# Delta rule of a hybrid decoder: two substitution steps a bank, merges of all heads and chunks at once, gate folded into the output norm

## The chip, the cores and the metric

One NeuronCore of one Trainium2 chip. The metric is the device time of one launch in microseconds, the median over several runs. The kernel is written in Bass with Tile: the author gives the order of the program, and Tile's scheduler places every instruction in its engine's queue, the earlier ones of the program first where several could go, and adds the semaphores. On the chip each engine works through its queue in that order.

## The reference

A decoder trunk of two layers, 256 tokens, width 1024, float32. A layer is a half-step SwiGLU, a mixer of three branches side by side, and another half-step SwiGLU. The mixer's branches are a forgetting attention (8 heads), a latent attention (8 heads) and a gated delta rule (8 heads of 64). The delta rule, per head and chunk of 64 tokens, cut to what matters here:

```
m     = strict_lower(k_beta @ k.T * decay)
t_inv = inverse of (I + m)              # unit lower triangle, 64 x 64
w, u  = t_inv @ (k_beta * exp(gc)), t_inv @ v_beta
o     = recurrence over the chunks with w, u and a 64 x 64 state
o     = rmsnorm(o, dn_o_norm) * silu(z)
x    += W_out(sig(gA) * (A @ W_A) + sig(gB) * (B @ W_B) + sig(gC) * (o @ W_C))
```

## The kernel before, in words

All weights come from HBM in pieces of 512 KB through `wchunk` (L158): SP starts the load of `raw` (L163), ScalarE rounds it to `hi` (L164), VectorE takes the rest `lo` (through `tt`, L98), and `mm_w` (L177 to L179) or `mm_t` (L188 to L190) multiplies with three matmuls. Three buffers each of `raw`, `hi` and `lo` rotate. PSUM has four banks `m` for the projections, two `g` for the delta rule and two `a` for the attention heads; `turned` (L216) transposes an activation with L221 and splits it.

The function `mixer` gives its program in this order. First come the small projection with the gates' logits, the delta rule's six pieces of q, k and v, the decay sums (L459 to L486), the short convolutions, the norms of q and k, and the matrices N (L565) and Q (L569) for 8 heads and two blocks of 128 tokens, each with two chunks of 64. N holds the strict triangle; the inverse is built in three sizes:

- Substitution (L596 to L605). The 16x16 diagonal blocks of all heads and blocks stand side by side in `cn`. Step j spreads row j of each block over its 16 partitions with two matmuls with a selector (L599, L600), and VectorE multiplies and subtracts. The selected rows come from a copy of N that the steps don't change. After 15 steps `uc` has the inverses, and L609 writes them, masked to block diagonals, into `Um`, one half by VectorE and one by GpSimd.
- Merge of 16 to 32 (L614 to L626). Four groups of four heads, one after the other: a 32x32 transpose on VectorE (L617), four 128x128 matmuls (L620), the mask `lev16`, four matmuls (L625), a subtraction.
- Merge of 32 to 64 (L627 to L642). Two blocks times two halves: a transpose (L632), eight 32x32 matmuls (L635) at one position of the array, a negated copy on ScalarE (L637), eight matmuls (L640) at another, and a copy (L642).

Then the loop over the two blocks (L650 to L701): products with the triangle (L663, L668, L672), the state (L681, L657), the output (L686), then its norm (L693 to L701): `s2` is scaled twice by `rq`, brought to mean plus epsilon, `rsqrt` (L144) takes three Newton rounds, and `odn` is scaled.

Behind the delta rule in the program stand the query and key projections of the forgetting attention (`wft` 6 to 9), its values (`win[1]`), the delta rule's output gate `zt` (`win[2]`, L718 to L727, on ScalarE, VectorE and GpSimd), the latent attention's projections, the forgetting attention (8 heads, `attention` L356), the gates of branch 0, the latent attention, the gates of branches 1 and 2, and the merges of the branches 0, 1 and 2. Right before branch 2, GpSimd multiplies `odn` by `zt` (L823, L824); its operand is then transposed by L221. Then come `W_out` and the second SwiGLU.

Of the kernel before, what the change touches and what calls it, by code (L numbers as in the profile page):

```python
# [12 lines left out]
AF = mybir.ActivationFunctionType  # L13
ALU = mybir.AluOpType
# [4 lines left out]
P = 128  # L19
# [14 lines left out]

C_ID = 0
C_LV = C_ID + P
C_TRI = C_LV + P
C_KR = C_TRI + P
C_SELC = C_KR + P
C_IDC = C_SELC + 16  # L40
C_BM = C_IDC + 16
C_M01 = C_BM + 8
C_SEL = C_M01 + 2
C_SC = C_SEL + 30
NC_ = C_SC + 3

PAIRS_1 = (0, 1, 2, 3, 4, 5)
PAIRS_2 = (6, 7, 8, 9, 2, 3)
# [6 lines left out]
def trunk(ctx, tc, x_in, pos_in, cst_in, msk_in, sel_in, vec_in, hv_in, onorm_in, fin_in, bg_in,  # L55
# [20 lines left out]
    def bank(tag):  # L76
        return psum_of[tag].tile([P, 512], F32, name="bank_" + tag)
# [4 lines left out]
    def held(name, dt=F32):  # L82
        return pair(PAIR[name], dt)

    def single(name, dt=F32):
        return big.tile([P, 1024], dt, name=name)

    def w2(shape=(P, 512)):
        return wk.tile(list(shape), F32, name="w2", bufs=NW2)

    def g2(shape=(P, 512), dt=F32):
        return wk.tile(list(shape), dt, name="g2", bufs=NG2)
# [4 lines left out]
    def tt(eng, o, a, b, op):  # L97
        eng.tensor_tensor(out=o, in0=a, in1=b, op=op)  # L98
# [4 lines left out]
    def ts(o, a, s1, op0, s2=None, op1=None, eng=None):  # L103
        k = dict(op1=op1) if op1 is not None else {}
        (eng or V).tensor_scalar(out=o, in0=a, scalar1=s1, scalar2=s2, op0=op0, **k)
# [11 lines left out]
    for l in range(1, L):  # L117
        nc.scalar.dma_start(vec[l], vec_in[l])
    cc = lambda o, n: cst[:, o:o + n]
    ident, lev16, tri = cc(C_ID, P), cc(C_LV, P), cc(C_TRI, P)  # L120
    krsel = cst[0:64, C_KR:C_KR + P]
    idc, bm, m01 = cc(C_IDC, 16), cc(C_BM, 8), cc(C_M01, 2)
    invf, phase, sgn = [cc(C_SC + i, 1) for i in range(3)]
    bfc = const.tile([P, 3 * P + 16], BF16, name="bfc")
    msk = w2()
# [73 lines left out]
    def proj_t(ps, src, xs, kt=KD, k0=0, first=True, last=True):  # L199
        for q in range(0, kt, 2):  # L200
            w = wchunk(src[:, q * 512:(q + 2) * 512], 2, 512)
            mm_t(ps, w, 0, xs, k0 + q, 2, first and q == 0, last and q + 2 == kt)

    def two(tag):
        return [bank(tag) for _ in range(2)]
# [140 lines left out]
    def heads(ap):  # L346
        return ap.rearrange("p (h e) -> p h e", e=64)

    def hb(col, n=8, rows=slice(0, P)):
        return col[rows, :, None].broadcast_to([rows.stop - rows.start, n, 64])  # L350
# [38 lines left out]
    def mixer(l, norm, next_norm):  # L389
# [141 lines left out]
        rq = small([P, 2, 8], "rq")  # L531
        ts(rq, of(rs, 1), 0.125, ALU.mult)


        ps = bank("g")
        for p in range(4):
# [37 lines left out]
        for c in range(2):  # L574
# [1 line left out]
            for p in range(4):  # L576
                nc.tensor.transpose(ps[:, p * P:(p + 1) * P], vT[:, p, c * P:(c + 1) * P], ident)
            tt(V, heads(vr[:, c, :]), heads(ps), hb(irk[:, c, :]), ALU.mult)
        Ub = held("U")
        Um = [four(Ub[:, c, :]) for c in range(2)]  # L580

        cu = g2((P, 2, 16, 16))
        cn, uc = cu[:, 0], cu[:, 1]
# [10 lines left out]
        tt(V, cnl, flat(cn), cnh.bitcast(F32), ALU.subtract)  # L594
        G.tensor_copy(uc, idc[:, None, :].broadcast_to([P, 16, 16]))
        for j in range(15):  # L596
            ps = bank("g")
            sel = sel16[:, j, :]
            nc.tensor.matmul(ps[:, 0:256], sel, cnh, start=True, stop=False)  # L599
            nc.tensor.matmul(ps[:, 0:256], sel, cnl, start=False, stop=True)  # L600
            n = 15 - j
            row = ps[:, 0:256].rearrange("p (t i) -> p t i", t=16)[:, :, j + 1:16]
            tmp = cn[:, :, 0:n]
            tt(V, tmp, row, uc[:, :, j:j + 1].broadcast_to([P, 16, n]), ALU.mult)
            tt(V, uc[:, :, j + 1:16], uc[:, :, j + 1:16], tmp, ALU.subtract)  # L605
        for c in range(2):
            o = Um[c].rearrange("p h (b i) -> p h b i", i=16)
            u = uc[:, 8 * c:8 * c + 8, None, :].broadcast_to([P, 8, 8, 16])
            tt(V if c == 0 else G, o, u, bm[:, None, :, None].broadcast_to([P, 8, 8, 16]), ALU.mult)  # L609


        groups = [(c, slice(4 * par, 4 * par + 4)) for c in range(2) for par in range(2)]
        tr32 = {}
        for c, hs in groups:  # L614
            U, N = Um[c][:, hs, :], Nm[c][:, hs, :]
            Tm = g2()
            V.transpose(Tm, U.rearrange("p h i -> p (h i)"))  # L617
            psB = four(bank("g"))
            for p in range(4):
                nc.tensor.matmul(psB[:, p, :], N[:, p, :], four(Tm)[:, p, :], start=True, stop=True)  # L620
            B = four(g2())
            tt(V, B, psB, lev16[:, None, :].broadcast_to([P, 4, P]), ALU.mult)
            psU = four(bank("g"))
            for p in range(4):
                nc.tensor.matmul(psU[:, p, :], B[:, p, :], U[:, p, :], start=True, stop=True)  # L625
            tt(V, U, U, psU, ALU.subtract)  # L626
        Tq, Bq = [g2().rearrange("p (t i) -> p t i", i=32) for _ in range(2)]  # L627
        for c in range(2):
            for a in (0, 64):
                r0, r1 = slice(a, a + 32), slice(a + 32, a + 64)  # L630
                tq, bq = Tq[:, 8 * c:8 * c + 8, :], Bq[:, 8 * c:8 * c + 8, :]
                V.transpose(tq[r0], Um[c][r0, :, r0])  # L632
                psB = bank("g")[:, 0:256].rearrange("p (h i) -> p h i", i=32)
                for t in range(8):
                    nc.tensor.matmul(psB[r1, t, :], Nm[c][r0, t, r1], tq[r0, t, :], start=True, stop=True,  # L635
                                     tile_position=(a, a + 32))
                nc.scalar.activation(bq[r1], psB[r1], AF.Copy, scale=-1.0)  # L637
                psU = bank("g")[:, 0:256].rearrange("p (h i) -> p h i", i=32)
                for t in range(8):
                    nc.tensor.matmul(psU[r0, t, :], bq[r1, t, :], Um[c][r1, t, r1], start=True, stop=True,  # L640
                                     tile_position=(a + 32, a))
                V.tensor_copy(Um[c][r0, :, r1], psU[r0])  # L642


        odn = vr
# [4 lines left out]
        for c in range(2):  # L650
# [9 lines left out]
            W, Y = g2(), g2()  # L660
            psY = bank("g")
            for h in range(H):
                nc.tensor.matmul(psY[lo64, hs(h)], Um[c][lo64, th(h), lo64], R[lo64, hs(h)], start=True, stop=True)  # L663
            nc.scalar.copy(Y[lo64, :], psY[lo64, :])
            tt(V, heads(W[lo64, :]), heads(psY[lo64, :]), hb(bk[:, c, :], rows=lo64), ALU.mult)
            psZ = bank("g")
# [2 lines left out]
            tt(V, Y[hi64, :], R[hi64, :], psZ[hi64, :], ALU.subtract)  # L669
            psX = bank("g")  # L670
            for h in range(H):
                nc.tensor.matmul(psX[hi64, hs(h)], Um[c][hi64, th(h), hi64], Y[hi64, hs(h)], start=True, stop=True)  # L672
            tt(V, heads(W[hi64, :]), heads(psX[hi64, :]), hb(bk[:, c, :], rows=hi64), ALU.mult)
            if c == 0:
                Wk = g2()
# [17 lines left out]
            nc.scalar.activation(sq, o, AF.Square)  # L693
            s2 = small([P, 8], "s2")
            V.tensor_reduce(out=s2, in_=heads(sq), axis=AX.X, op=ALU.add)
            for _ in range(2):
                tt(V, s2, s2, rq[:, c, :], ALU.mult)
            ts(s2, s2, 1.0 / 64.0, ALU.mult, EPS, ALU.add)
            f = rsqrt(s2, [P, 8], "o")
            tt(V, f, f, rq[:, c, :], ALU.mult)  # L700
            tt(V, heads(o), heads(o), hb(f), ALU.mult)  # L701


        fqk, fvo = held("fqk"), held("fvo")
# [9 lines left out]
        proj_t(ps, win[1], xs)  # L714
        for b in range(2):
            nc.scalar.activation(fv[:, b, :], ps[b], AF.Copy, scale=rcol[:, b:b + 1])

        zt = single("zt").rearrange("p (b f) -> p b f", b=2)  # L718
        ps = two("m")
        proj_t(ps, win[2], xs)  # L720
        for b in range(2):
            nc.scalar.activation(zt[:, b, :], ps[b], AF.Copy, scale=rcolh[:, b:b + 1])
        for b in range(2):
            t = w2()
            nc.scalar.activation(t, zt[:, b, :], AF.Tanh)
            stt(zt[:, b, :], t, 1.0, zt[:, b, :], ALU.add, ALU.mult)
            tt(G, heads(zt[:, b, :]), heads(zt[:, b, :]), ong[:, None, :].broadcast_to([P, 8, 64]), ALU.mult)  # L727


        sl = small([P, 2, 2], "sl")  # L730
        junk = w2()
# [88 lines left out]
        gt1, gt2 = gates(1), gates(2)  # L820
        merge(0, op0, gt0)
        merge(1, operand(1, omla), gt1)
        for b in range(2):  # L823
            tt(G, odn[:, b, :], odn[:, b, :], zt[:, b, :], ALU.mult)  # L824
        tap("odn", odn)
        merge(2, operand(2, odn), gt2)
        yp = [parts(PAIR[f"y{i}"]) for i in range(2)]
# [82 lines left out]
def _constants():  # L910
    c = np.zeros((P, NC_), np.float32)
    i = np.arange(P)
    c[:, C_ID:C_ID + P] = np.eye(P)
    bi, bj = i[:, None] // 16, i[None, :] // 16
    c[:, C_LV:C_LV + P] = (bi % 2 == 1) & (bj == bi - 1)
    c[:, C_TRI:C_TRI + P] = i[None, :] >= i[:, None]
    for m in range(P):
        c[m % 32, C_KR + m] = 1.0
        c[32 + m % 32, C_KR + m] = 1.0
    for m in range(16):  # L920
        c[[m, 32 + m, 64 + m], C_SELC + m] = 1.0
    c[i, C_IDC + i % 16] = 1.0
    c[i, C_BM + i // 16] = 1.0
    c[:, C_M01] = (i // 16) % 2 == 0
    c[:, C_M01 + 1] = (i // 16) % 2 == 1
    c[:64, C_SEL + 14] = 1.0
    c[64:, C_SEL + 15] = 1.0
    half = 16
    invf = (np.float32(10000.0) ** (-np.arange(half, dtype=np.float32) / np.float32(half))).astype(np.float32)
    c[:, C_SC] = invf[i % 16]  # L930
    c[:, C_SC + 1] = np.where((i // 32) % 2 == 0, 0.25, 0.0)
    c[:, C_SC + 2] = np.where(((i // 32) % 2 == 1) & ((i % 32) < 16), -1.0, 1.0)
    return c
# [69 lines left out]
```

## Time and profile before

| what | us |
|---|---|
| median of 3 runs | 1421.68 |
| lowest and highest | 1421.5 and 1423.4 |
| the profiled execution, its time | 1423.29 |
| the profiled execution, its span | 1421.5 |

The profile is of one execution. Times are from the start of its first instruction. PE is TensorE, PEld its weight loads, DVE VectorE, ACT ScalarE, POOL GpSimd. Matmuls are pipelined, so the record of one is longer than the distance to the next one's start. A float32 matmul with plain float32 operands leaves two records. The granted clock is the share of TensorE's full clock: 1.00 is 2.4 GHz, 0.50 is 1.2 GHz, and what lies between is a mix of both within a stretch.

### The profile page before, as it was taken

How to read it: one execution, taken by the hardware profiler on the slowest of the kernel's cores; microseconds unless marked ns; L12 is line 12 of the kernel's file. 1: busy time of each engine (PE TensorE's matmuls, PEld its weight loads, DVE VectorE, ACT ScalarE, POOL GpSimd, SP SyncE). 2: the span in 40 equal slices, each digit the busy share in tenths (PEclk: the TensorE clock that was granted, in tenths of full speed). 3: DMA queues.
4: the chain of work that ended last, by engine and by line, in shares of the span. 5: the costliest groups of instructions: out<-in, count | busy, mean ns of one | idle time of the engine just before them, and what ended most of it. 6: DMA issues, size and time to landing. Idle time of an engine off the chain costs nothing.

```text
span 1421.5 us, 19541 instructions
## 1 busy us (share of the span) xinstructions
PE 1381.3 (97%) x7480; PEld 1158.8 (82%) x7480; DVE 941.6 (66%) x1575; ACT 661.8 (47%) x980; POOL 47.9 (3%) x39
## 2 busy tenths in 40 slices
PE   7999999999999999999999999999999997999996
PEld 6888889878888788888888888997788875888885
DVE  7866559778767766665566655885977665665654
ACT  5544445464443354444444444554544432544442
POOL 0000000000000400000000000000000013000000
PEclk9999999999999999999999999999999998999999
DMA  7555666524433356556655666554144323555563
GB/s 233 182 189 182 194 200 193 174 80 127 139 129 112 119 163 194 187 182 193 185 185 182 188 188 187 179 177 145 60 149 133 127 75 104 181 188 189 182 193 103
DMA packets 65436, 230.00 MB, mean 162 GB/s; under 512 B 8000, under 2 KB 8256, under 8 KB 65344
## 3 DMA queue, kind: packets, MB, share of 16 engines
q1 hardware_dynamic: 63760, 227.50, 51.2%
q10 hardware_dynamic: 1584, 1.26, 0.3%
q8 instruction: 58, 0.95, 0.3%
q14 instruction: 34, 0.28, 0.1%
HBM read 227.69 MB, written 1.05 MB: 161 GB/s over the span
## 4 chain that ended last, share of the span: by engine, by line
PE 61%; DVE 3%; issue 0%; ACT 0%; POOL 0%; DVEq 0%; POOLq 0%; ACTq 0%
PE bank_m L189 17%; PE bank_m L188 17%; PE bank_m L190 17%; PE bank_m L177 2%; PE bank_m L179 2%; PE bank_m L178 2%; PE bank_a L221 1%; PE bank_g L221 1%; DVE d L101 1%; DVE lo L98 1%; PE bank_a L361 0%; PE bank_a L380 0%; PE bank_a L360 0%; PE bank_g L686 0%; PE bank_g L620 0%
## 5 line engine op out<-in xcount | busy, mean ns | idle before, releaser
L98 DVE TENSOR_TENSOR lo<-raw,hi 128x1024 fp32r<-128x1024 f32 x422 | 522.3, 1239 | 336.8 <-ACT hi L164 326.2
L164 ACT CAST hi<-raw 128x1024 fp32r<-128x1024 f32 x422 | 443.4, 1052 | 509.3 <-PE bank_m L189 413.3
L188 PE MATMUL bank_m<-hi,xs 128*128 128x512 f32 x992 | 388.7, 394 | 1.1 <-ACT hi L164 1.1
L189 PE MATMUL bank_m<-hi,xs 128*128 128x512 f32 x992 | 389.7, 393 | 0.0
L190 PE MATMUL bank_m<-lo,xs 128*128 128x512 f32 x992 | 369.1, 395 | 0.0
L188 PEld LDWEIGHTS bank_m<-hi,xs 128*128 128x128 f32 x992 | 186.8, 188 | 38.9 <-ACT hi L164 1.5
L189 PEld LDWEIGHTS bank_m<-hi,xs 128*128 128x128 f32 x992 | 187.0, 188 | 38.4 <-issue 0.4
L190 PEld LDWEIGHTS bank_m<-lo,xs 128*128 128x128 f32 x992 | 186.8, 188 | 37.5
L189 PE MATMUL bank_m<-hi,d 128*128 128x512 f32 x516 | 203.1, 394 | 2.0 <-DVE d L98 2.0
L188 PE MATMUL bank_m<-hi,d 128*128 128x512 f32 x516 | 201.2, 398 | 1.0 <-ACT d L225 0.9
L190 PE MATMUL bank_m<-lo,d 128*128 128x512 f32 x516 | 189.7, 393 | 0.0
L189 PEld LDWEIGHTS bank_m<-hi,d 128*128 128x128 f32 x516 | 97.7, 189 | 22.2 <-DVE d L98 2.5
L188 PEld LDWEIGHTS bank_m<-hi,d 128*128 128x128 f32 x516 | 97.2, 190 | 22.1 <-ACT d L225 2.0
L190 PEld LDWEIGHTS bank_m<-lo,d 128*128 128x128 f32 x516 | 97.6, 189 | 20.1
L177 PE MATMUL bank_m<-xs,hi 128*128 128x256 f32 x320 | 90.3, 283 | 0.0
L178 PE MATMUL bank_m<-xs,hi 128*128 128x256 f32 x320 | 90.1, 283 | 0.0
L179 PE MATMUL bank_m<-xs,lo 128*128 128x256 f32 x320 | 89.4, 284 | 0.0
L179 PEld LDWEIGHTS bank_m<-xs,lo 128*128 128x128 f32 x320 | 60.8, 192 | 1.0 <-issue 0.3
L177 PEld LDWEIGHTS bank_m<-xs,hi 128*128 128x128 f32 x320 | 61.4, 192 | 0.1
L178 PEld LDWEIGHTS bank_m<-xs,hi 128*128 128x128 f32 x320 | 61.4, 192 | 0.0
L330 ACT ACTIVATE w<-bank_m,hr 128x512 f32<-128x512 f32 (+1 forms) x48 | 31.4, 655 | 29.3 <-PE bank_m L190 27.2
L101 DVE SCALAR_TENSOR_TENSOR w<-w,bank_m 128x512 f32<-128x512 f32 (+1 forms) x48 | 30.7, 640 | 15.5 <-ACT w L330 15.4
(280 smaller groups left out, 1263.5 us busy)
## 6 DMA issues: line engine op xcount, KB each, us to landing
raw<-in_gu_dram SPq DMA_DIRECT2D x176, 512.0 KB, 4.4
raw<-in_dw_dram SPq DMA_DIRECT2D x88, 512.0 KB, 3.6
raw<-in_win_dram SPq DMA_DIRECT2D x72, 512.0 KB, 3.9
raw<-in_wft_dram SPq DMA_DIRECT2D x40, 512.0 KB, 4.0
raw<-in_br_dram SPq DMA_DIRECT2D x24, 512.0 KB, 3.6
raw<-in_wo_dram SPq DMA_DIRECT2D x16, 512.0 KB, 3.9
bias<-in_bg_dram SPq DMA_DIRECT2D x12, 256.0 KB, 3.4
raw<-in_uq_dram SPq DMA_DIRECT2D x4, 512.0 KB, 3.7
```

Of the source, the lines that this page charges most:

```text
L98: eng.tensor_tensor(out=o, in0=a, in1=b, op=op)
L101: V.scalar_tensor_tensor(out=o, in0=a, scalar=s, in1=b, op0=op0, op1=op1)
L164: nc.scalar.copy(hi[:, :n], raw[:, :n])
L177: nc.tensor.matmul(o, wh[:, k, cs], h, start=first and i == 0, stop=False)
L178: nc.tensor.matmul(o, wh[:, k, cs], l, start=False, stop=False)
L179: nc.tensor.matmul(o, wl[:, k, cs], h, start=False, stop=last and i == len(order) - 1)
L188: nc.tensor.matmul(ps[b], h, wh[:, k, cs], start=first and k == 0, stop=False)
L189: nc.tensor.matmul(ps[b], l, wh[:, k, cs], start=False, stop=False)
L190: nc.tensor.matmul(ps[b], h, wl[:, k, cs], start=False, stop=last and k == kt - 1)
L221: nc.tensor.transpose(ps[:, j * T + b * P:j * T + (b + 1) * P], src(b)[:, (q + j) * P:(q + j + 1) * P], ident)
L330: nc.scalar.activation(t, psg[b][:, 0:n], AF.Tanh, scale=hr[:, b:b + 1])
```

## The change

- Substitution: one bank of `g` holds the selected rows of two steps, so a bank is taken for every second step. The matmuls and VectorE's operations stay.
- Merge of 16 to 32: only the diagonal 32x32 blocks are kept, for all 8 heads and both blocks of 128 tokens in one tile of 128x512. One transpose, 64 matmuls of 32x32 that go round the four diagonal positions of the array, a mask `low32`, 64 more matmuls, and a subtraction in the right half.
- Merge of 32 to 64: one transpose, ScalarE writes the diagonal blocks into `U64` (64 columns a head), 32 matmuls that alternate between two positions, two negated copies (ScalarE and VectorE), 32 matmuls, two copies.
- The projection and activation of `zt` stands right after the merges, ahead of the loop over the blocks and so ahead of the forgetting attention's projections.
- The norm: instead of scaling by `rq` twice before and once after the root, epsilon is divided by the square of the scale (`erq`, once), and `odn` is multiplied by `zt` on VectorE right after its norm. The two GpSimd products before branch 2 go.

```diff
+        erq = small([P, 2, 8], "erq")
+        ts(erq, of(ss, 1), 64.0 * EPS, ALU.mult)
...
-        Ub = held("U")
-        Um = [four(Ub[:, c, :]) for c in range(2)]
+        U64 = held("U")[:, 0, :].rearrange("p (t i) -> p t i", i=64)
...
         for j in range(15):
-            ps = bank("g")
-            sel = sel16[:, j, :]
-            nc.tensor.matmul(ps[:, 0:256], sel, cnh, start=True, stop=False)
-            nc.tensor.matmul(ps[:, 0:256], sel, cnl, start=False, stop=True)
+            if j % 2 == 0:
+                ps = bank("g").rearrange("p (s x) -> p s x", s=2)
+                for i in range(2 if j < 14 else 1):
+                    for u, part in enumerate((cnh, cnl)):
+                        nc.tensor.matmul(ps[:, i, :], sel16[:, j + i, :], part, start=u == 0, stop=u == 1)
             n = 15 - j
-            row = ps[:, 0:256].rearrange("p (t i) -> p t i", t=16)[:, :, j + 1:16]
+            row = ps[:, j % 2, :].rearrange("p (t i) -> p t i", t=16)[:, :, j + 1:16]
...
+        U32 = g2()
+        Uv = by32(U32)
+        for i in range(2):
+            ts(Uv[:, :, 16 * i:16 * i + 16], uc, m01[:, i:i + 1], ALU.mult)
+        Tm, Bm = g2(), by32(g2())
+        V.transpose(Tm, U32)
+        psB = by32(bank("g"))
+        for g in range(16):
+            for q, r in enumerate(quarter):
+                nc.tensor.matmul(psB[r, g, :], Nm[g // 8][r, g % 8, r], by32(Tm)[r, g, :], start=True, stop=True,
+                                 tile_position=(32 * q, 32 * q))
+        tt(V, Bm, psB, low32[:, None, :].broadcast_to([P, 16, 32]), ALU.mult)
+        psU = by32(bank("g"))
+        for g in range(16):
+            for q, r in enumerate(quarter):
+                nc.tensor.matmul(psU[r, g, :], Bm[r, g, :], Uv[r, g, :], start=True, stop=True,
+                                 tile_position=(32 * q, 32 * q))
+        tt(V, Uv[:, :, 16:32], Uv[:, :, 16:32], psU[:, :, 16:32], ALU.subtract)
+        Tm = g2()
+        V.transpose(Tm, U32)
+        for i in range(2):
+            nc.scalar.activation(U64[:, :, 32 * i:32 * i + 32], Uv, AF.Copy, scale=even32[:, i:i + 1])
+        psB = by32(bank("g"))
+        Bm = by32(g2())
+        for g in range(16):
+            for a in (0, 2):
+                r0, r1 = quarter[a], quarter[a + 1]
+                nc.tensor.matmul(psB[r1, g, :], Nm[g // 8][r0, g % 8, r1], by32(Tm)[r0, g, :], start=True, stop=True,
+                                 tile_position=(32 * a, 32 * a + 32))
+        nc.scalar.activation(Bm[quarter[1]], psB[quarter[1]], AF.Copy, scale=-1.0)
+        ts(Bm[quarter[3]], psB[quarter[3]], -1.0, ALU.mult)
+        psU = by32(bank("g"))
+        for g in range(16):
+            for a in (0, 2):
+                r0, r1 = quarter[a], quarter[a + 1]
+                nc.tensor.matmul(psU[r0, g, :], Bm[r1, g, :], Uv[r1, g, :], start=True, stop=True,
+                                 tile_position=(32 * a + 32, 32 * a))
+        nc.scalar.copy(U64[quarter[0], :, 32:64], psU[quarter[0]])
+        V.tensor_copy(U64[quarter[2], :, 32:64], psU[quarter[2]])
...
             s2 = small([P, 8], "s2")
             V.tensor_reduce(out=s2, in_=heads(sq), axis=AX.X, op=ALU.add)
-            for _ in range(2):
-                tt(V, s2, s2, rq[:, c, :], ALU.mult)
-            ts(s2, s2, 1.0 / 64.0, ALU.mult, EPS, ALU.add)
+            stt(s2, s2, 1.0 / 64.0, erq[:, c, :], ALU.mult, ALU.add)
             f = rsqrt(s2, [P, 8], "o")
-            tt(V, f, f, rq[:, c, :], ALU.mult)
             tt(V, heads(o), heads(o), hb(f), ALU.mult)
+            tt(V, o, o, zt[:, c, :], ALU.mult)
...
         merge(0, op0, gt0)
         merge(1, operand(1, omla), gt1)
-        for b in range(2):
-            tt(G, odn[:, b, :], odn[:, b, :], zt[:, b, :], ALU.mult)
         tap("odn", odn)
         merge(2, operand(2, odn), gt2)
```

The removed lines of the old merges are L606 to L642 as described above. The ten lines of `zt` are moved unchanged. The constants change with it: `low32` (32 columns) for `lev16`, `even32` for the block mask.

## Rows read from the trace of the kernel before

**Rows 1.** The page's first part: busy time of each engine, share of the span.
```profile
PE 1381.3 (97%) x7480; PEld 1158.8 (82%) x7480; DVE 941.6 (66%) x1575; ACT 661.8 (47%) x980; POOL 47.9 (3%) x39
```
**Rows 2.** Windows: length; PE, PEld, DVE, ACT, POOL busy; clock; DMA share, GB/s.
```profile
450.00:460.00 10.00, 9.18 (x84) 7.96 (x83) 8.35 (x27) 2.35 (x7) 1.27 (x1) 0.83 0.15 54
...
1170.00:1180.00 10.00, 1.07 (x6) 0.58 (x4) 8.64 (x17) 1.04 (x1) 5.76 (x5) 0.82 0.53 171
1180.00:1190.00 10.00, 9.54 (x32) 7.57 (x33) 2.56 (x3) 2.22 (x3) 0.37 (x1) 0.67 0.03 13
```
**Rows 3.** Timeline of PE, second layer's merges: start, length, line; idle and releaser in brackets.
```profile
1155.95 0.39 PE L386 MATMUL bank_a<-d,pt 128*128 128x64 f32 x2
...
1170.79 0.27 PE L221 MATMUL bank_a<-cst,dnv 128*128 128x128 f32 x1
1180.43 1.54 PE L221 MATMUL bank_a<-cst,dnv 128*128 128x128 f32 x6 [9.36 <-POOL dnv L98]
...
1190.67 0.39 PE L188 MATMUL bank_m<-hi,d 128*128 128x512 f32 x1
1190.89 0.39 PE L189 MATMUL bank_m<-hi,d 128*128 128x512 f32 x1
```
**Rows 4.** Timelines of DVE and POOL, the last steps of `odn` (named dnv there).
```profile
1178.25 0.69 DVE L98 TENSOR_TENSOR dnv<-dnv,rs_yo 128x512 f32<-128x512 f32 x1
...
1179.11 1.26 POOL L98 TENSOR_TENSOR dnv<-dnv,zt 128x512 f32<-128x512 f32 x1 [2.33 <-DVE dnv L98]
```
**Rows 5.** Timeline of PE, first layer, the same transposes.
```profile
472.04 0.55 PE L221 MATMUL bank_a<-cst,dnv 128*128 128x128 f32 x3 [0.69 <-POOL dnv L98]
```
**Rows 6.** Timeline of DVE, second layer: first substitution step, first merge's transpose.
```profile
1018.50 0.40 DVE L98 TENSOR_TENSOR g<-bank_g,g 128x240 f32<-128x240 f32 x1
...
1060.43 0.70 DVE L617 STREAM_TRANSPOSE g<-d 128x512 f32<-128x512 f32 x1
```
**Rows 7.** Timeline of PE, second layer, the first merge's two products.
```profile
1064.49 1.05 PE L620 MATMUL bank_g<-g,d 128*128 128x128 f32 x8
...
1070.38 1.05 PE L625 MATMUL bank_g<-d,g 128*128 128x128 f32 x8
```
**Rows 8.** Waits, 1000 to 1200 us: who for whom, us in all, times, longest.
```profile
DVE g L98 <- PE bank_g L600: 4.7, 8, 0.9
```
**Rows 9.** Lines 620 and 635: records, ns least/median/most, first and last start us.
```profile
L620 PE MATMUL bank_g<-g,d x64: 270/275/328, 369.3 to 1086.8; 128*128 128x128 f32 x64
...
L635 PEld LDWEIGHTS bank_g<-g,d x128: 101/108/108, 397.1 to 1110.5; 32*32 32x32 f32 x128
```
**Rows 10.** Timeline of PE, second layer: bursts of 32x32 records, the triangle's first use.
```profile
1110.05 0.19 PE L640 MATMUL bank_g<-d,g 32*32 32x32 f32 x1
1110.08 0.19 PE L635 MATMUL bank_g<-g,d 32*32 32x32 f32 x1
1110.08 0.19 PE L640 MATMUL bank_g<-d,g 32*32 32x32 f32 x1
1110.11 0.19 PE L635 MATMUL bank_g<-g,d 32*32 32x32 f32 x1
1110.11 0.19 PE L640 MATMUL bank_g<-d,g 32*32 32x32 f32 x1
...
1116.17 0.69 PE L640 MATMUL bank_g<-d,g 32*32 32x32 f32 x16
1116.78 1.14 PE L663 MATMUL bank_g<-dnv,d 64*64 64x64 f32 x16
```
**Rows 11.** Lines 360 and 364: first products of the forgetting attention's heads, columns as rows 9.
```profile
L360 PE MATMUL bank_a<-d x32: 272/373/579, 257.9 to 1066.0; 64*128 64x128 f32 x32
...
L364 PE MATMUL bank_a<-parts_b,bfc x16: 229/230/232, 299.8 to 1066.7; 96*128 96x128 bf16 x16
```
**Rows 12.** Timeline of PE, second layer, the second block's state and output products.
```profile
1145.75 1.95 PE L657 MATMUL bank_g<-state,d 128*128 128x128 f32 x16
...
1162.25 1.89 PE L686 MATMUL bank_g<-g,d 128*128 128x64 f32 x16
```

## Prediction before the run

> **What bounds the kernel now.** The first view is the page's busy table [rows 1]: TensorE is busy for 97% of the span and VectorE for 66%. So almost everything off TensorE is hidden, and a change can pay in two ways only: less TensorE work in a stretch that is full, or less waiting in a stretch that is not. The second view, the windows of 10 us [rows 2], finds the stretches that are not full. In the second layer's mixer, from 1170 to 1180 us, TensorE works 1.07 us of 10 at a granted clock of 0.82, and from 1180 to 1190 us the clock is 0.67. The first layer has a weaker spot, 450 to 460 us, clock 0.83. The third view, the timeline of TensorE, says what the big hole is [rows 3]. The last head of the latent attention ends at 1155.95 us plus 0.39. The merge of that branch then runs until the transpose at 1170.79 us, and then nothing until 1180.43 us, when the transposes of `odn` (the delta rule's output) start, after 9.36 us of idle that GpSimd's product ended. One step back [rows 4]: VectorE scales `odn` at 1178.25 us, GpSimd multiplies it by `zt` at 1179.11 us for 1.26 us. The delta rule is the last chain to arrive. In the first layer the same wait is 0.69 us [rows 5]: there the chain comes just in time.
>
> **How long the chain is, and where.** In the second layer the substitution starts at 1018.50 us [rows 6], the first 32x32 transpose of the merges at 1060.43 us [rows 6], and the product that uses the finished triangle (L663) at 1116.78 us [rows 10]. So the substitution with the masking takes 42 us, the merges 56 us, and the chunk loop with its norm the other 64 us up to 1180.4. The steps are short and the waits long: the first merge's transpose is done at 1061.13 us, its TensorE step starts at 1064.49 us, and the next one at 1070.38 us [rows 6, 7], because TensorE executes in the order in which it was given the projections and heads between.
>
> **The change, part by part, for each of the two layers.**
>
> Two substitution steps a bank. The 30 matmuls stay, and each bank of the two of pool `g` now holds two rows, so up to four steps can be selected ahead. VectorE waited for L600 8 times, 4.7 us in all, in the second layer [rows 8]. I take 4 us off the chain, bounds 0 and 4.7. TensorE: no change.
>
> The merges of 16. Removed: 32 matmuls of 128x128, in the trace 64 records a layer (128 in both lines' x64 over two layers, [rows 9] has the first line); eight records run in 1.05 us of which the last one's tail is 0.27 [rows 7, 9], so 0.111 us each and 7.1 us in all. Added: 128 matmuls of 32x32, two records each, 256 records. The merges of 32: 64 matmuls, 128 records, before and after, but the new order alternates between two positions of the array instead of staying on one.
>
> What does a 32x32 record cost? On one position, 16 records take 0.69 us with a tail of 0.19 [rows 10]: 0.033 us each. So removed work is 7.1 + 128 x 0.033 = 11.3 us. If the new records ran one after the other, they would take 384 x 0.033 = 12.7 us, 1.4 more than now. But where a burst of L640 meets one of L635, on other rows and columns of the array, the two go side by side: five records start between 1110.05 and 1110.11 us [rows 10], 0.015 us apart. Two side by side make 384 x 0.033 / 2 = 6.3 us, 5.0 less than now. If all four positions of the merge of 16 ran together, it would be 256 x 0.033 / 4 + 128 x 0.033 / 2 = 4.2 us, 7.1 less. I take two side by side, as that is the row that shows it; bounds +1.4 and -7.1 a layer. The Trainium skill (TensorEngine Tiling (Array Packing), Instruction Overhead) speaks against small pieces: each matmul has about 60 cycles of overhead, however few its columns. At 2.4 GHz that is 25 ns, an estimate of 384 x 0.025 = 9.6 us and a gain of 1.7 us a layer where the other sentences have 5.0; the records 0.015 us apart don't bear that floor out, but they are few.
>
> Of the TensorE work saved, not all comes off the end. Around the merges TensorE is full, so the projections behind them start earlier; but the mixer's end hangs on the last attention head too. Heads are paced both by full TensorE and by their own steps. I take half of 2 x 5.0 us: 5.0 us for the kernel, bounds -2.8 (slower) and 14.2.
>
> The chain through the merges. Before, four groups went through transpose, product, mask, product, subtract, then four blocks through four steps each. Now one pass: two masked copies, transpose, product, mask, product, subtract, transpose, product, negated copy, product, copy. That is 12 steps. Own times: seven on VectorE or ScalarE at 0.69 to 0.70 us or less [rows 4, 6], one more transpose, and four bursts on TensorE of 1.0 to 4.2 us; 10 to 18 us. Waits: four handings to TensorE at 3.4 us as above, and some eight others at about 1 us; 22 us. Together 32 to 40 us against 56. With the 4 us from the substitution and the saved mask, the chain gets 20 to 28 us shorter. The hole needs 9.4.
>
> VectorE's work falls (the big mask, eight operations of 0.69 and four transposes of 0.70 go, about six of these come back, and two products move over from GpSimd at about 0.69 instead of 1.26 us): no term at 66% busy. The norm's three small operations a chunk go, and the product at the end stays on one engine; of the 2.2 us between 1178.25 and 1180.43 us [rows 3, 4] about 1 us would go. This is inside the hole and counts nothing again.
>
> The gate `zt`, moved ahead. Its projection (four weight loads on SP's queue, their four casts on each of ScalarE and VectorE, 48 matmuls at 0.22 us, the distance of the last two of [rows 3], 10.6 us; two copies, two tanh, two combinations, two GpSimd products) now stands before the query, key and value projections of the forgetting attention: 12 weight loads, with their casts and matmuls, come out that much later, on SP's queue too. Nothing is added. The first head's logits start at 257.9 us but its decay part starts at 299.8 us [rows 11], 41.9 us later, held by the decay sums, not by the projections. So 10.6 us is covered: 0. Without that cover it would cost 10.6 us a layer.
>
> **The sum.** The second layer's wait, 9.4 us. Behind it the clock: the two windows [rows 2] hold (1 - 0.82) x 2 x 10 + (1 - 0.67) x 2 x 10 = 10.2 us at the lower of the two levels, after TensorE had stood still; of these 6.2 come after the 1180.4 restart, so 3.1 us of work lost. The first layer's wait, 0.7. TensorE work, 5.0. Together 18.2 us. The profiled execution took 1423.29 us (span 1421.5 and 1.8 around it), 1.6 above the median of the three runs; from it 1405.1, from the median **1403.5**. What is late next: the latent attention's last heads, then the branch merges without a stop.
>
> **The rivals.** (1) *The attention's tail becomes the bound.* Today the delta rule's second chunk fills the gaps of the last heads with TensorE work: L657 1.95 us, three bursts like L663 at 1.14, L686 1.89 [rows 10, 12], 7.3 us with tails, some 6.8 without. If this runs earlier and no head moves, those gaps stay open in both layers and 13.6 us of the 18.2 are given back: 1417. For it: from 1145 us on no projection is left. Against it: the projections that the delta work would displace last longer into the tail. (2) *Everything lands:* four positions together and all of it off the end: 9.4 + 3.1 + 0.7 + 14.2 = 27.4, so 1394. For it: TensorE is full around the merges. Against it: the heads' own pace. (3) *Slower:* changing the position on every matmul exposes the weight load, 0.108 us a record [rows 9], which now hides behind the record before. 2 x 384 x 0.108 = 82.9 us against 22.6 removed, less 13.2 for the holes: +47, so 1469. It decides from (22.6 + 13.2) / 768 = 0.047 us a record on. Against it: the change from L640 to L635 in rows 10 shows no such step. (4) *The chain doesn't shorten:* one long pass waits at TensorE as often as four overlapping groups did, and only 2 us of TensorE work comes off: 1420. Against it: 12 steps instead of some 20 in a row.
>
> **How the numbers follow.** Forecast 0.60; rival 1 0.17; rival 2 0.09; rival 3 and other losses of order 0.06; rival 4 0.08. A measurement of this kernel can tell some 0.2%, 2.8 us, from no change. Forecast, rivals 1 and 2 are faster: 0.86. Rival 4 is mostly within: 0.08. Slower 0.06. The range runs from rival 2 to rival 1: 1394 to 1417.
>
> **What would show it.** In the changed profile the idle before the `odn` transposes is gone in both layers, and the windows behind it have a full clock. The first use of the triangle comes 20 us or more sooner after the substitution's start. The 32x32 records start 0.016 us or less apart. The forecast is wrong if TensorE's idle shows up around the last heads instead (rival 1), if the bursts take over 0.033 us a record (rival 3), or if the wait for `odn` is still there (rival 4).

## The result and the profile after

The changed kernel takes 1403.95 us (median of four executions, 1401.79 to 1406.7), the kernel before 1422.54 (1421.5 to 1436.14) on the same chip: a ratio of 0.9845, 95% interval 0.9803 to 0.9887. The forecast was 1403.5. It is met, but as a sum in which errors cancel, and the trace shows them.

The page of the changed kernel, first part:

```profile
PE 1367.7 (98%) x7864; PEld 1146.8 (82%) x7864; DVE 922.2 (66%) x1543; ACT 663.0 (47%) x980; POOL 39.0 (3%) x33
```

The span is 1401.1 us, 20.4 shorter than before. TensorE's busy time is 13.6 us less than in [rows 1], although it has 384 records more; only 6.8 us of the gain is idle time gone. That is not the split that was forecast (9.4 + 0.7 of idle, 5.0 of work).

The windows of the changed kernel, columns as in [rows 2]:

```profile
440.00:450.00 10.00, 7.61 (x53) 6.64 (x52) 7.60 (x24) 3.96 (x8) 0.00 (x0) 1.00 0.40 127
450.00:460.00 10.00, 7.90 (x41) 6.38 (x39) 4.68 (x16) 3.27 (x11) 0.00 (x0) 0.74 0.08 31
460.00:470.00 10.00, 9.46 (x41) 7.83 (x41) 2.60 (x6) 3.62 (x8) 0.00 (x0) 0.75 0.01 2
...
1130.00:1140.00 10.00, 7.90 (x61) 6.61 (x60) 8.06 (x25) 3.55 (x8) 0.00 (x0) 0.87 0.31 107
1140.00:1150.00 10.00, 8.16 (x32) 6.47 (x31) 3.35 (x13) 2.79 (x10) 0.00 (x0) 0.50 0.00 0
1150.00:1160.00 10.00, 9.22 (x49) 7.46 (x49) 3.85 (x9) 3.73 (x9) 0.00 (x0) 0.95 0.00 0
1170.00:1180.00 10.00, 8.37 (x41) 6.59 (x39) 8.06 (x8) 3.68 (x5) 5.81 (x5) 1.00 0.73 234
```

From 1170 to 1180 us TensorE was busy for 1.07 us of 10 and is now for 8.37: the hole is closed. In its place each layer has a thin stretch earlier on, in the windows from 450 and from 1130 us, and the clock falls to 0.74 and 0.50 (0.50 is the lower level, 1.2 GHz). The timeline of TensorE there, second layer (start, length; idle and releaser in brackets):

```profile
1137.92 1.15 PE L381 MATMUL bank_a<-cst,pr 128*128 128x128 f32 x3 [2.10 <-ACT pr L374]
...
1143.03 1.15 PE L381 MATMUL bank_a<-cst,pr 128*128 128x128 f32 x3 [1.29 <-ACT pr L374]
...
1147.38 1.05 PE L381 MATMUL bank_a<-cst,pr 128*128 128x128 f32 x3 [0.54 <-DVE d L98]
...
1151.64 0.80 PE L381 MATMUL bank_a<-cst,pr 128*128 128x128 f32 x3 [0.55 <-DVE d L98]
...
1159.82 0.38 PE L222 MATMUL bank_a<-cst,dnv 128*128 128x128 f32 x2
```

The last row is the transposes of `odn` that stood at 1180.43 us behind 9.36 us of idle [rows 3]; now nothing is waited for. The four rows above are the last heads of the latent attention: TensorE has nothing left to put between them and waits, for ScalarE's exponentials before the first two and for a product of VectorE before the last two, 4.5 us in all (4.8 in the first layer). The last head itself hardly moves: its last product starts at 1153.7 us, before at 1156.1. This is rival 1's picture.

The chain of the delta rule, second layer: on VectorE the first substitution step, the first merge's transpose and the last two products of `odn`; then on TensorE the triangle's first use.

```profile
1023.00 0.40 DVE L98 TENSOR_TENSOR g<-bank_g,g 128x240 f32<-128x240 f32 x1
...
1046.25 0.71 DVE L619 STREAM_TRANSPOSE g<-g 128x512 f32<-128x512 f32 x1
...
1139.42 0.69 DVE L98 TENSOR_TENSOR dnv<-dnv,rs_yo 128x512 f32<-128x512 f32 x1
1140.15 0.69 DVE L98 TENSOR_TENSOR dnv<-dnv,zt 128x512 f32<-128x512 f32 x1
```

```profile
1077.83 1.14 PE L685 MATMUL bank_g<-dnv,d 64*64 64x64 f32 x16
```

From first step to first transpose: 23.3 us, before 41.9 [rows 6]. From there to the triangle's use: 31.6, before 56.4 [rows 6, 10]. `odn` is ready at 1140.8 us, 19 us before TensorE asks for it. And the bursts of 32x32 records, TensorE in the first layer:

```profile
356.31 1.29 PE L623 MATMUL bank_g<-g,d 32*32 32x32 f32 x128
362.79 1.29 PE L629 MATMUL bank_g<-g,g 32*32 32x32 f32 x128
369.71 1.20 PE L641 MATMUL bank_g<-g,d 32*32 32x32 f32 x64
```

With the last record's 0.19 us [rows 10] taken off, 128 records on four positions take 1.10 us, 8.6 ns each; 64 on two take 1.01, 16 ns each. So all positions of a burst run side by side. Two bursts of each kind come to 4.2 us a layer against 11.3 removed: 7.1 saved, the outer bound of the prediction.

**The account.** Low clock counts with half its length, since half the work is lost. The landmark is the first transpose of `y` behind the branch merges: 489.3 us and 1195.2 us before, 487.6 and 1177.1 after.

| us gained | first layer | second layer |
|---|---|---|
| TensorE work of the merges | 7.1 | 7.1 |
| waits gone: `odn` 0.69, a chunk product 0.67; `odn` 9.36, a head 1.42, the N matrices 1.13 and 0.92 | 1.4 | 12.8 |
| idle in the tail of the heads | -4.8 | -4.5 |
| low clock: 3.4 to 10.2 us; 17.0 to 13.7 us | -3.4 | 1.7 |
| sum | 0.3 | 17.1 |
| measured at the landmark | 1.7 | 16.4 |

The remaining 2.3 of the 20.4 us come behind the second layer's landmark, where the clock now doesn't fall at 1200 us. Of the first layer's 1.4 us of difference, 0.4 is waits at its N matrices (1.0 and 0.2 us) that are gone, against a new one of 0.8; the rest is not accounted for. Against 14.2 us less of TensorE work stand 9.3 us of new idle between the heads.

### The profile page after: what moved, and what is told of

It reads as the page before. It is cut to its first block, busy times and chain, and to the rows that moved or that the text cites. A ratio compares the mean times of both kernels' runs of the same rounds, so it can differ in the third digit from the quotient of the medians.

```text
span 1401.1 us, 20260 instructions
## 1 busy us (share of the span) xinstructions
PE 1367.7 (98%) x7864; PEld 1146.8 (82%) x7864; DVE 922.2 (66%) x1543; ACT 663.0 (47%) x980; POOL 39.0 (3%) x33
```

## The experiments

**How they are compared.** The time of one program varies by several us with the length of the low clock: the changed kernel gave 1401.79 to 1406.7 us on one chip and 1405.7 to 1412.83 on another. Each run lists span and mean granted clock, so the lost work is span x (1 - clock); the time less this is called the full-clock time here. It agrees within 1 to 4 us among the runs of most kernels here (6.3 for the one-position kernel below, 7.5 for the kernel before). Its medians: before 1404.5, 1404.4 and 1403.0 beside three groups of experiments; the changed kernel 1387.8, 1383.9 when run again and 1389.1 as a third program with the same queues (the last experiment), so that less than some 5 us between two groups says nothing. The clock is listed to 0.001, which is 1.4 us. The measure takes the low clock out as if it were chance; two experiments below show that it isn't wholly.

**The merges alone.** The kernel before with the new merges; steps, gate and norm as they were.

```diff
-        for c, hs in groups:
...
+        for g in range(16):
+            for q, r in enumerate(quarter):
+                nc.tensor.matmul(psB[r, g, :], Nm[g // 8][r, g % 8, r], by32(Tm)[r, g, :], start=True, stop=True,
+                                 tile_position=(32 * q, 32 * q))
...
```

> The kernel before with the new merges alone: one substitution step a bank, the gate's projection behind the values, the old norm and the product on GpSimd stay. Theory (the merges' length made the delta rule's output late, the rest is covered): the hole of 9.4 us before the odn transposes in the second layer is gone and the time is 1402 to 1408 us. Rival (the short norm and the two-step banks carry a good part): the chain is still late by some us, 1410 to 1416 us.

Measured: 1411.01 us, ratio 0.9887 (0.9842 to 0.9932); full clock 1387.1. The time is in the rival's range, but the hole is gone as the theory had it; the transposes of `odn` have no idle before them:

```profile
1167.57 0.60 PE L222 MATMUL bank_a<-cst,dnv 128*128 128x128 f32 x4
```

At full clock the merges alone bring all that the whole change brings (1383.9 to 1389.1 in its runs and a repeat further down); the rest of the difference is low clock, 20.5 us of it from 995 to 1016 us. The transpose-to-triangle stretch is 31.3 us, as in the changed kernel, and the substitution keeps most of its length (38.9 us, before 41.9).

**All but the merges.** The changed kernel with the merges of before.

```diff
-        by32 = lambda t: t.rearrange("p (t i) -> p t i", i=32)
...
+        for c, hs in groups:
+            U, N = Um[c][:, hs, :], Nm[c][:, hs, :]
+            Tm = g2()
+            V.transpose(Tm, U.rearrange("p h i -> p (h i)"))
...
```

> The changed kernel with the old merges (four groups, then four blocks, block-diagonal tiles); two-step banks, the moved gate and the short norm stay. Theory: the chain gets some 4 us shorter in the substitution and 1 to 2 us at the norm, so some 4 of the 9.4 us of idle stay, and TensorE saves nothing: 1414 to 1420 us. Rival (the end of the chain is what counts): the hole is gone without the merges too, 1404 to 1408 us.

Measured: 1406.21 us, ratio 0.9842 (0.9803 to 0.9881); full clock 1395.3. The triangle's first use is at 1108.18 us, only 8.6 before that of [rows 10], and still `odn` isn't waited for (TensorE of this kernel, no idle in brackets):

```profile
1108.18 1.14 PE L685 MATMUL bank_g<-dnv,d 64*64 64x64 f32 x16
...
1164.38 0.60 PE L225 MATMUL bank_a<-cst,dnv 128*128 128x128 f32 x4
```

So the hole doesn't need the short merges. What this version lacks is the 14.2 us less of TensorE work, and of these 6 to 11 come off the end: 1395.3 against 1383.9 to 1389.1 at full clock. Its heads' tail holds some 4 us of idle, the changed kernel's 9.3.

**The same records, one position at a time.** Loops exchanged, nothing else.

```diff
-        for g in range(16):
-            for q, r in enumerate(quarter):
+        for q, r in enumerate(quarter):
+            for g in range(16):
...
```

> The changed kernel with the loops of the merges' matmuls swapped: all 16 of one position of the array first, then the next position, so that the 32x32 records run one after the other. By the trace of the changed kernel the bursts of 128 records take 1.1 us and of 64 records 1.0 us; one after the other at 0.032 us a record they would take 4.1 and 2.0 us, 8 us more of TensorE work a layer. If TensorE's work around the merges reaches the end: 1404 + 16 = 1420 us. If the latent attention's last heads set the mixer's end and the work only fills their gaps: 1404 to 1408 us. I expect the second, with 1406 us.

Measured: 1426.09 us, ratio 0.9971 (0.9947 to 0.9995); full clock 1402.7. TensorE, first layer:

```profile
356.92 3.93 PE L623 MATMUL bank_g<-g,d 32*32 32x32 f32 x128
366.04 4.58 PE L629 MATMUL bank_g<-g,g 32*32 32x32 f32 x128
378.65 2.11 PE L641 MATMUL bank_g<-g,d 32*32 32x32 f32 x64
385.81 2.11 PE L649 MATMUL bank_g<-g,g 32*32 32x32 f32 x64
```

In the second layer the second burst takes 3.93 us as well:

```profile
1073.06 3.93 PE L629 MATMUL bank_g<-g,g 32*32 32x32 f32 x128
```

So a layer takes 12.1 us against 5.0 (the three rows of the changed kernel and one more of 1.2), 14.2 more in all; the first layer's 4.58 us are longer because a stretch of 6.8 us at the lower clock begins at 368.9 us, within that burst. The full-clock time grows by 14 to 19. The idea that the thin tail would swallow the added work fell: what is added to the changed kernel's TensorE work around the merges reaches the end in full. With the two loops in this order nearly the whole gain of the change is gone, though TensorE doesn't wait for `odn` here either: what the closed hole gives goes for the most part into the tail's idle (4.8 and 4.0 us) and the dearer merges.

**The gate's move alone.** The kernel before with `zt` computed where the change puts it.

```diff
+        zt = single("zt").rearrange("p (b f) -> p b f", b=2)
...
         odn = vr
...
-        zt = single("zt").rearrange("p (b f) -> p b f", b=2)
...
```

> The kernel before with the gate's projection moved ahead of the loop, and nothing else changed. If the move carries a part of the gain by itself, as the runs without the new merges (1406 us) and with them alone (1411 us) suggest: the chain starts 10 us earlier, the second layer's hole of 9.4 us closes, 1405 to 1412 us. If the move is neutral: 1420 to 1424 us.

Measured: 1412.73 us, ratio 0.9888 (0.9852 to 0.9925); full clock 1397.7. The triangle's use comes later than before (1122.4 us), and yet the transposes of `odn` stand without a wait, 1.0 us after GpSimd's product is done:

```profile
1165.72 0.60 PE L221 MATMUL bank_a<-cst,dnv 128*128 128x128 f32 x4
```

VectorE shows a part of how. The norm of the second block, here:

```profile
1158.27 0.69 DVE L707 TENSOR_REDUCE s<-g 128x8 f32<-128x512 f32 x1 [0.42 <-ACT g L705]
...
1159.60 0.17 DVE L147 TENSOR_SCALAR rs_yo<-s 128x8 int32<-128x8 int32 x1
1159.81 0.17 DVE L149 TENSOR_SCALAR rs_yo<-rs_yo 128x8 int32<-128x8 int32 x1
...
1162.56 0.69 DVE L98 TENSOR_TENSOR dnv<-dnv,rs_yo 128x512 f32<-128x512 f32 x1
```

and in the kernel before, VectorE first, then GpSimd:

```profile
1165.56 0.69 DVE L695 TENSOR_REDUCE s<-g 128x8 f32<-128x512 f32 x1 [0.70 <-ACT g L693]
...
1169.32 0.80 DVE L147 TENSOR_SCALAR rs_yo<-s 128x8 int32<-128x8 int32 x1
1170.16 1.20 DVE L149 TENSOR_SCALAR rs_yo<-rs_yo 128x8 int32<-128x8 int32 x1
1171.28 1.21 DVE L98 TENSOR_TENSOR lo<-raw,hi 128x1024 fp32r<-128x1024 f32 x1
...
1175.59 1.22 DVE L101 SCALAR_TENSOR_TENSOR rs_yo<-rs_to,rs_yo 128x8 f32<-128x8 f32 x1
```

```profile
1168.81 2.53 POOL L98 TENSOR_TENSOR d<-d,d 128x512 f32<-128x512 f32 x2 [14.18 <-DVE s L105]
1173.25 3.54 POOL L98 TENSOR_TENSOR d<-d,d 128x512 f32<-128x512 f32 x2 [1.91 <-DVE d L101]
```

From the reduction to the end of the scaling it takes 5.0 us here and 13.4 before [rows 4]: there the small steps stood behind the weight casts and gate combinations on VectorE, and those that ran beside a GpSimd addition took 0.8 to 1.2 us instead of 0.17. In the changed kernel the norm takes 4.4 us (1135.74 to 1140.11). The chunk loop is shorter as well: from the triangle's first use to the end of the second block's output product 34.4 us here, 47.4 before. So the loop gives 12.9 us and the norm 8.4, against 5.6 for the later triangle; the hole was 9.36. Why the loop and the norm both stand closer when the gate's projection moves is not shown.

**The steps alone, and the norm alone,** one execution each, beside a before of 1428.67 us (median).

```diff
+            if j % 2 == 0:
+                ps = bank("g").rearrange("p (s x) -> p s x", s=2)
+                for i in range(2 if j < 14 else 1):
...
```

```diff
-            for _ in range(2):
-                tt(V, s2, s2, rq[:, c, :], ALU.mult)
...
+            stt(s2, s2, 1.0 / 64.0, erq[:, c, :], ALU.mult, ALU.add)
...
-            tt(G, odn[:, b, :], odn[:, b, :], zt[:, b, :], ALU.mult)
+            tt(V, odn[:, b, :], odn[:, b, :], zt[:, b, :], ALU.mult)
```

> The kernel before with two substitution steps a bank and nothing else. My term: 4 us off the chain, so of the second layer's 9.4 us before the odn transposes some 5 stay. Rival: with more selected rows ready the chain's steps still wait their turn on VectorE, and the hole stays at 8 to 10 us.

> The kernel before with the short norm, and the product with the gate on VectorE instead of GpSimd at its old place in the program; nothing else. My term: about 1 us off the end of the chain, 8 us of the hole stay. Rival: the end of the chain was stretched by GpSimd (VectorE's small operations take up to 1.2 us there instead of 0.17), so more goes, and the hole falls to 5 us or less.

Measured: 1421.12 us (full clock 1394.2) and 1428.52 (1394.3). In neither does TensorE wait for `odn`; at full clock both gain about the hole (8.8 us against 1403.0). Both had a clock of half from 304 to 331 us, where the before that is profiled has 1.00 throughout; the steps alone, windows as above:

```profile
300.00:310.00 10.00, 8.96 (x46) 6.98 (x45) 9.52 (x36) 6.23 (x27) 2.89 (x3) 0.69 0.20 66
310.00:320.00 10.00, 10.00 (x42) 7.85 (x41) 5.68 (x17) 2.84 (x8) 0.00 (x0) 0.50 0.00 0
320.00:330.00 10.00, 10.00 (x41) 8.78 (x41) 5.21 (x17) 3.54 (x9) 0.00 (x0) 0.50 0.00 0
```

and another such stretch at 1007 to 1017 us (1010 to 1031 with the norm alone). A slow TensorE could give the other engines' chain time to catch up, so neither trace can say that its edit closed the hole. The times say a little more: four of the seven executions of the kernel before beside them had the same mean clock as the steps alone, 0.981, and took 1427.3 to 1431.2 us, 6 to 10 us more. But it is one execution of each edit. What the first does size is the substitution, by VectorE's first step and first transpose:

```profile
1028.85 0.41 DVE L98 TENSOR_TENSOR g<-bank_g,g 128x240 f32<-128x240 f32 x1 [0.21 <-issue]
...
1058.24 0.69 DVE L618 STREAM_TRANSPOSE g<-d 128x512 f32<-128x512 f32 x1
```

29.4 us, and 27.4 in the first layer. With the old merges behind, two steps a bank give 25.8 to 29.4 us (this run and the one without the new merges, both layers), one step a bank 33.9 to 41.9 (before and the gate's move alone): about 10 us, by the means of four each. More than VectorE's listed waits can show: they are idle time only. In the second layer's substitution VectorE was idle for 9 us in the kernel before and for 3 in the changed one, and did 24 and 11 us of other work there; the steps themselves take 8.7 us in either.

**The gate put back.** The changed kernel with `zt` behind the chunk loop and its product before the third branch.

```diff
-            tt(V, o, o, zt[:, c, :], ALU.mult)
...
+        for b in range(2):
+            tt(V, odn[:, b, :], odn[:, b, :], zt[:, b, :], ALU.mult)
...
```

> The changed kernel with the gate's projection back behind the values of the forgetting attention (VectorE's product with it stands right before branch 2 instead of in the loop). Prediction on record (the move costs and gains nothing): 1404 us, within 2 us. Rival, from the traces so far (in the kernels with the moved gate the matrices N start 10 us earlier and the second layer has no idle and no low clock around 994 to 1004 us; in the kernels without it both are there): 1409 to 1414 us.

> The changed kernel once more, beside the next three on the same chip: about 1404 us, the yardstick for them.

Measured: 1407.79 us, ratio 0.9862 (0.9783 to 0.9942), full clock 1385.3, and the changed kernel beside it 1409.63, ratio 0.9872 (0.981 to 0.9933), full clock 1383.9. The move costs nothing and, with the other parts there, gains nothing that these runs can tell. One thing goes with the place: the clock where the second layer's N matrices start. The gate put back, then the kernel before:

```profile
990.00:1000.00 10.00, 10.00 (x47) 7.91 (x47) 9.00 (x30) 3.05 (x14) 3.21 (x3) 0.50 0.11 42
```

```profile
990.00:1000.00 10.00, 8.87 (x56) 7.13 (x55) 7.90 (x17) 7.92 (x26) 3.17 (x3) 0.83 0.35 111
1000.00:1010.00 10.00, 8.89 (x56) 6.93 (x55) 8.99 (x38) 3.74 (x12) 0.05 (x1) 0.83 0.00 0
```

All five profiles with the gate behind have a wait of TensorE of 1.1 us at these matrices and behind it a low clock between 990 and 1031 us, 6.8 to 20.5 us long; the eight with the gate in front have neither there. The same changed kernel, second execution, windows of the tail:

```profile
450.00:460.00 10.00, 8.27 (x35) 6.71 (x34) 3.83 (x14) 2.78 (x10) 0.00 (x0) 0.52 0.01 6
460.00:470.00 10.00, 9.46 (x36) 7.64 (x36) 1.51 (x5) 3.01 (x7) 0.00 (x0) 0.63 0.01 2
...
1140.00:1150.00 10.00, 8.16 (x32) 6.56 (x31) 4.39 (x15) 3.26 (x11) 0.00 (x0) 0.50 0.00 0
1150.00:1160.00 10.00, 9.46 (x40) 7.78 (x39) 2.33 (x7) 2.27 (x7) 0.00 (x0) 0.65 0.00 0
```

Same work, same waits in the tail, but the clock is low for 17.1 us in each layer instead of 10.2 and 13.7. Over the whole span the low clock costs some 5 us more than the first time, more than the 2.5 us by which this span is longer.

**Filling the tail.** `odn` is ready 19 us before it is used, so its branch could be merged before the latent attention's. First the order alone, then also with its operand's transposes in banks of pool `g`.

```diff
-        merge(1, operand(1, omla), gt1)
         tap("odn", odn)
         merge(2, operand(2, odn), gt2)
+        merge(1, operand(1, omla), gt1)
```

```diff
-            turned(lambda b: o[:, b, :], op, 4, "a")
+            turned(lambda b: o[:, b, :], op, 4, "g" if i == 2 else "a")
...
```

> The changed kernel with the delta rule's branch merged before the latent attention's (0, 2, 1 instead of 0, 1, 2): its operand is ready about 10 us before the last head. Theory (the attention's tail is the bound now; it holds 4.8 and 4.5 us of idle of TensorE and 10.2 and 13.7 us at the lower clock level): the merge's 11 us of matmuls fill the tail in both layers, idle and low clock there go, 1384 to 1394 us. Rival (the tail's cost is hidden elsewhere or the weights come too late): 1401 to 1406 us.

> The branch order 0, 2, 1 again, with the operand of branch 2 transposed in the two banks g of the delta rule, which are free by then, instead of the banks a, which the heads hold. In the run before, the odn transposes stood behind the last head's banks (461.7 us, after the tail). Theory: now they go at about 453 us and the merge fills the tail of the heads: idle and low clock there mostly go, 1386 to 1396 us. Rival: the weights' buffers or TensorE's order keep it behind the heads, 1402 to 1406 us.

Measured: 1405.39 us, ratio 0.9838 (0.9802 to 0.9874), full clock 1391.6; and 1404.29, ratio 0.9845 (0.9776 to 0.9915), full clock 1391.0. Neither gains. TensorE of the first, first layer, shows the transposes still among the last heads, whose banks they share:

```profile
461.72 1.06 PE L222 MATMUL bank_a<-cst,dnv 128*128 128x128 f32 x4
```

With banks of their own they come at 446 to 454 us and fill the tail, but the last head slips from 462.4 us in the changed kernel to 470.85, and new waits follow it, 1.9 us in all; TensorE of the second:

```profile
453.27 1.39 PE L222 MATMUL bank_g<-cst,dnv 128*128 128x128 f32 x6
...
470.85 0.33 PE L385 MATMUL bank_a<-d,pt 128*128 128x64 f32 x2
473.13 0.66 PE L222 MATMUL bank_a<-cst,d 128*128 128x128 f32 x4 [0.66 <-DVE d L98]
```

What the work fills in one place is missing behind the last head, where the latent attention's own merge has nothing beside it.

**The gate projection of the first branch held back** until the heads are given out.

```diff
-        gt0 = gates(0)
...
-        gt1, gt2 = gates(1), gates(2)
+        gt0, gt1, gt2 = gates(0), gates(1), gates(2)
```

> The changed kernel with one line moved: the gates of branch 0 stand behind the latent attention in the program instead of ahead of it, so that the heads go before them and all three gates are left to fill TensorE. In the changed kernel the last head ends some 16 us after the last filler in the first layer, with 4.8 us of idle and 10 to 17 us at the lower clock, and about the same in the second. Theory (what is left of the mixers' loss is this tail, and it opens because filler runs out before the heads): the heads end before the filler, idle and low clock at the tail go, 1384 to 1394 us. Rival (the heads are slow of themselves, or the transposes of the operands wait in their place): 1400 to 1406 us.

Measured: 1404.53 us, ratio 0.983 (0.9802 to 0.9857), full clock 1389.1. The engines' queues came out the same as in the changed kernel, so the question was not answered; the run stands as a repeat of the changed kernel. No version tried here is clearly faster than the changed kernel.

## Why the prediction was right, and where it wasn't

- *The second layer's wait, 9.4, and the first's, 0.7:* gone in both layers, as forecast. The reason given, that the chain through steps and merges must get shorter, is too narrow: the gate's move alone closes it with the triangle 5.6 us later, because the loop and the norm behind the triangle get 21.3 us shorter. The prediction read VectorE's last two steps before the hole [rows 4] and not the ten us ahead of them.
- *The chain, 20 to 28 us shorter:* 43.5 (98.3 to 54.8, first step to triangle). The merges came out at 31.6 against 32 to 40. The term that failed is the substitution's 4 us, read as VectorE's waits for L600 [rows 8] with 4.7 as upper bound. With two steps a bank it is about 10 us shorter by the runs with old merges, so the sum of waits named for one releaser was no bound: it leaves out the time in which VectorE does something else between two steps.
- *TensorE work, 5.0:* the records were priced too dear. "Two side by side" should have been all positions of a burst (7.1 a layer, 14.2 in both, rival 2's figure). The half that was to come off the end was taken without a row behind it: against the version with the old merges 6 to 11 of the 14.2 us come off, and against the account's 14.2 stand 9.3 of idle in the tail, which leaves 4.9: near the forecast's 5.0, but not by its working. The estimate from the Trainium skill (TensorEngine Tiling (Array Packing), Instruction Overhead), 25 ns a record, does not agree with the trace: 8.6 ns a record, or 17 ns for a matmul of two records.
- *The clock, 3.1:* nothing. The low clock behind the hole went, but the tails and the end of the program took it back (30.0 us low before and 31.6 after over the span, half of which counts: 0.8 us lost).
- *Rival 1:* its mechanism is there in both layers, with 9.3 us of idle instead of 13.6. Rival 2's work and rival 1's tail came together, and the forecast had taken them as alternatives. That the sum still came to 1403.5 is luck to that extent: 9.2 us more from TensorE and some 4 us more of waits gone, against 9.3 of new idle and 3.9 on the clock.
- *Gate at 0:* right as a cost, also when put back, though the cover was not whole: the first head's decay part starts at 305.3 us, 5.5 later than in [rows 11]. What the forecast didn't list is that the move by itself closes the hole, some 7 us at full clock. *Rival 3:* no exposed weight load; the rotation of positions is what makes the records short. *Rival 4:* the chain did shorten.

## What to carry to other kernels

Several parts of a change that each close the same hole don't add; look first at what is queued on the engine that ends it, since here the merges alone, the gate's move alone and everything but the merges each closed it. Work taken off a full TensorE came off the end only in part here, some 6 to 11 of 14.2 us, while idle opened around the attention's heads. Small fp32 matmuls on independent positions of the array belong in an order that changes the position each time: the same 384 records cost 5.0 us in turn and 12.1 us position by position. Where the granted clock varies, compare times less span x (1 - clock), or a part worth 5 us is lost in it; and expect that work pulled forward leaves a thin stretch behind where TensorE idles and its clock falls.

## What was not expected of the hardware

- 32x32 fp32 records on four positions start 8.6 ns apart, on two 16 ns, against 33 ns on one [rows 10].
- The one-position kernel is the only one whose clock falls around the merges, for 17 us in three stretches from 368.9, 1065.2 and 1085.7 us. The other falls in the mixers of the thirteen profiles come shortly after TensorE stood idle; before these three it had no idle, and worked on these bursts among other things. No run tells why.
- A program's low clock moves from execution to execution: 1405.7 to 1412.83 us for the changed kernel in one group of runs at mean clocks of 0.985 to 0.979, with the same work.
- The kernels with the steps alone and the norm alone had 27.3 us of half clock in the first layer, at a place where no other profile here has more than 3.4, and no hole in the second. That the slow TensorE gave the chain time is one reading of these two; that the kernel before at the same mean clock was 6 to 10 us slower than the steps alone speaks for the edit itself. It was not tested by itself.
- VectorE operations on 128x8 that take 0.17 us took 0.80 to 1.22 us while GpSimd added 128x512 tiles. That the two get in each other's way is read from these rows; it was not tested by itself.
